# Moving the general expert path: from before the first four of experts, unrolled, to between the fourth and fifth four, as a loop

## The chip, the cores and the metric

The kernel runs on one core of one Trainium2 chip. The metric is the device time of one execution in microseconds (us); three runs of the kernel before gave 936.14, 939.47 and 940.57, median 939.47.

## The reference

A batch of one sequence with 256 tokens of 1024 features passes through two blocks. The first is sparse attention and a gated MLP, merged and projected by `w_out`, and then a mixture of 32 experts:

```
gp = softmax(h @ rg_w + rg_b)                   # best of 4 groups
el = (h @ re_w + re_b)[group]                   # 2 best of its 8 experts
for e in range(32):
    he = silu(h @ w_gate[e]) * (h @ w_up[e])    # 1024 -> 256
    y = y + comb[:, e] * (he @ w_down[e])       # 256 -> 1024
x = rms_norm(x + y)
```

The second block (two layers, each with a gated linear recurrence and a chunked mLSTM) follows on the same `x`. All data is float32. The expert weights alone are 32 x 3 x 1 MiB, read once.

## The kernel before

Only the stage of the experts matters here. The 32 experts are worked through as eight fours, numbered q = 0 to 7 as in the code (so the fourth and fifth four of the title are four 3 and four 4). Each expert of a four has 32 slots for tokens, so a four fills the 128 partitions. For each four:

- `onehot(q)` (L976 to L982, VectorE) writes `oht`, the one-hot matrix that says which token sits in which slot. Its tile has the tag `sOH` and two buffers.
- `gather(q)` (L1027, 32 matmuls) multiplies the tokens `h2h` and `h2l` by `oht`; L1031 and L1032 put the result into `xg`.
- `hidden(q)` (L1129, 64 matmuls with 512 columns on 32-column tiles) multiplies `xg` by the gate and up weights; L1131 and L1132 make `sil`. L1116 to L1120 make the slot weights on VectorE.
- `output(q)` transposes `sil` (L1140), multiplies by the down weights (L1149, 32 matmuls) and scatters into `x1` (L1156 on TensorE, L1158 on VectorE).

The loop at the end writes these as hidden(q), a condition, gather(q + 1), output(q). A scheduler orders each engine's instructions inside a straight piece, so gather(q + 1) and output(q) are interleaved, but nothing moves across a condition. The condition after hidden(q) (L1166, L1167) asks whether an expert of the four has more than 32 tokens; if so, the same four is worked through again with the slots from 32 on. On these inputs that happens once, after hidden(2).

The general path stands ahead of four 0 (L1047 to L1090): if an expert has more than 64 tokens (`CAP`), all 32 experts are applied to the left-over tokens, in code that is unrolled 32 times. Its weight tiles `wf` have the tag `sOH` too. On these inputs no expert has so many tokens: every engine jumps over it. Of a condition each engine has its own branch, and the way past it has a short block of its own, in which the engine raises its semaphores by what the skipped code would have raised them. In SP's block there are eight such steps, one for each of the eight semaphores (lanes, named DMAHW0 to DMAHW7) that its transfers count on in turn; each step waits for the count of all the transfers issued so far on its lane.

The weights are loaded on one queue, SP's, as transfers of 512 KiB. 19 buffers of 1 MiB are used in turn; a four takes 8 for gate and up and 4 for down. `eloads(12 * q + 27)` after the condition of four q refills the 8 buffers that hidden(q) has read, `eloads(12 * q + 31)` after output(q) the 4 of the down weights: 24 transfers in all. They keep the order of the program on SP, and SP's branches stand among them. A transfer is issued when the one eight before it has landed (same lane) and its buffer is free. The 8 buffers of the gate and up weights count as free once TensorE is past the condition of four q, since the repeated four reads them as well. After the last four, `head_load` (L251) loads the first weight chunk of the next block and ScalarE and VectorE split it (L273, L274); that split stands ahead of the last four's output on ScalarE.

Of the kernel before, what the change touches and what calls it, by code (L numbers as in the profile page):

```python
# [19 lines left out]
KT = 8  # L20
# [159 lines left out]
def model(ctx, tc, A, out, dbg=None):  # L180
# [10 lines left out]
    def nm(s):  # L191
        uid[0] += 1
        return f"{s}_{uid[0]}"

    def psum(tag="mm", bufs=4):
        return pp.tile([P, 512], F32, tag=tag, name=nm(tag), bufs=bufs)
# [4 lines left out]
    def psum_t():  # L201
        return psum("tp", 2)

    def f32(ap):
        return ap.bitcast(F32)
# [15 lines left out]
    def vc(name, j=0, n=1):  # L221
        o, _ = _VEC[name]
        return vec[:, o + j:o + j + n]
# [269 lines left out]
    with tc.tile_pool(name="b1", bufs=1) as bp, tc.tile_pool(name="sp1", bufs=3) as sp:  # L493
# [383 lines left out]
        def x1k(i):  # L877

            return x1[:, i, :].rearrange("t (p k) -> t k p", k=KT)
# [85 lines left out]
    with moe, tc.tile_pool(name="mo", bufs=1, reuse_waits="tile") as bp:  # L965
# [53 lines left out]
        def gather(oht, afters=None):  # L1019


            pss = [psum() for _ in range(2)]
            for i in range(2):
                with tc.issue_after(afters[i].ins) if afters else ExitStack():
                    for k in range(KT):
                        for n, part in enumerate((h2h, h2l)):
                            TE.matmul(pss[k // 4][:, P * (k % 4):P * (k % 4) + P], lhsT=part[i][:, k, :], rhs=oht[:, i, :],  # L1027
                                      start=i + n + k % 4 == 0, stop=i + n + k % 4 == 5)
            xg = bp.tile([P, KT, P], F32, tag="xg", name=nm("xg"), bufs=2)
            for k in range(4):  # L1030
                S.activation(out=xg[:, k, :], in_=pss[0][:, P * k:P * k + P], func=AF.Copy, scale=vc("n2gp", k))  # L1031
            V.tensor_tensor(out=xg[:, 4:8, :], in0=pss[1][:].rearrange("p (k t) -> p k t", k=4),  # L1032
                            in1=vc("n2gp", 4, 4).rearrange("p (k o) -> p k o", o=1).to_broadcast([P, 4, P]), op=OP.mult)
            return xg
# [9 lines left out]
        while folds:  # L1044
            ada_fold()

        over = nc.values_load(ovi[0:1, 0:1], min_val=0, max_val=2 * T)  # L1047
        with tc.If(over > CAP):
            cw = bp.tile([P, 256], F32, tag="ohx", name="cw")[:, 0:64].rearrange("p (i e) -> p i e", i=2)
            for i in range(2):  # L1050
                V.tensor_scalar(out=tmp[:, i, :], in0=oh1[:, i, :], scalar1=s4[:, i, 2:3], scalar2=None, op0=OP.mult)
                V.scalar_tensor_tensor(out=cw[:, i, :], in0=oh2[:, i, :], scalar=s4[:, i, 3:4], in1=tmp[:, i, :], op0=OP.mult, op1=OP.add)
            V.tensor_tensor(out=cw, in0=cw, in1=ovm, op=OP.mult)
            hfT = [bp.tile([P, KT, P], F32, name=nm("hfT"), **at) for at in (dict(tag="xg", bufs=2), dict(tag="bc"))]
            for i in range(2):
                for k4 in range(2):
                    pt = psum_t()
                    for k in range(4):
                        TE.transpose(pt[:, k * P:(k + 1) * P], x1k(i)[:, 4 * k4 + k, :], ident)
                    for k in range(4):  # L1060
                        V.tensor_scalar(out=hfT[i][:, 4 * k4 + k, :], in0=pt[:, k * P:(k + 1) * P], scalar1=vc("n2gp", 4 * k4 + k), scalar2=None, op0=OP.mult)
            for e in range(NEXP):
                gus = [psum(), psum()]
                for g, w in enumerate((A["w_gate"], A["w_up"])):
                    for kq in range(4):
                        wf = bp.tile([P, 2, FF], F32, tag="sOH", name=nm("wf"), bufs=2)
                        SY.dma_start(out=wf, in_=w[0, e].rearrange("(p k) c -> p k c", k=KT)[:, 2 * kq:2 * kq + 2, :])
                        for i in range(2):
                            for k in (2 * kq, 2 * kq + 1):
                                TE.matmul(gus[i][:, 256 * g:256 * g + 256], lhsT=hfT[i][:, k, :], rhs=wf[:, k % 2, :], start=k == 0, stop=k == KT - 1)  # L1070
                heTs = []
                for i, gu in enumerate(gus):
                    sil = bp.tile([P, T], F32, tag="sil", name=nm("sil"), bufs=2)
                    S.activation(out=sil, in_=gu[:, 0:256], func=AF.Silu, scale=r2[:, i, 3:4])
                    V.scalar_tensor_tensor(out=sil, in0=gu[:, 256:512], scalar=cw[:, i, e:e + 1], in1=sil, op0=OP.mult, op1=OP.mult)
                    pt = psum_t()
                    for f in range(2):
                        TE.transpose(pt[:, f * P:(f + 1) * P], sil[:, f * P:(f + 1) * P], ident)
                    heT = bp.tile([P, T], F32, tag="heT", name=nm("heT"), bufs=2)
                    V.tensor_copy(heT, pt[:, 0:256])  # L1080
                    heTs.append(heT)
                for n in range(4):
                    wf = bp.tile([P, 2, 256], F32, tag="sOH", name=nm("wf"), bufs=2)
                    SY.dma_start(out=wf, in_=A["w_down"][0, e].rearrange("(f p) c -> p f c", p=P)[:, :, 256 * n:256 * n + 256])
                    for i in range(2):
                        po = psum()
                        for f in range(2):
                            TE.matmul(po[:, 0:256], lhsT=heTs[i][:, f * P:(f + 1) * P], rhs=wf[:, f, :], start=f == 0, stop=f == 1)
                        xs = x1[:, i, 256 * n:256 * n + 256]
                        V.tensor_tensor(out=xs, in0=xs, in1=po[:, 0:256], op=OP.add)  # L1090


        bc = bp.tile([P, 5, T], F32, name="bc")
        s5 = bp.tile([5, T], F32, name="s5")
        pt = psum_t()
# [10 lines left out]
        def hidden(b, xg):  # L1106

            q4, keep = b % NQ, tc.keep_in_program_order if not b else lambda r: r
            ws = loaded["g", q4]

            slot = cc("slot")[:, b:b + 1]
            oa = bp.tile([P, T], F32, tag="oa", name=nm("oa"))
            ohs = bp.tile([P, T], F32R, tag="ohs", name=nm("ohs"), bufs=3)
            wsl = bp.tile([P, 3], F32, tag="wsl", name=nm("wsl"), bufs=2)
            for j in range(2):
                V.scalar_tensor_tensor(out=oa, in0=bc[:, j, :], scalar=slot, in1=bc[:, 2 + j, :], op0=OP.is_equal, op1=OP.mult, accum_out=wsl[:, j:j + 1])  # L1116
            V.tensor_tensor(out=wsl[:, 0:1], in0=wsl[:, 0:1], in1=wsl[:, 1:2], op=OP.add)
            V.tensor_scalar(out=oa, in0=bc[:, 0, :], scalar1=slot, scalar2=None, op0=OP.is_equal)
            V.scalar_tensor_tensor(out=ohs, in0=bc[:, 1, :], scalar=slot, in1=oa, op0=OP.is_equal, op1=OP.add)
            V.scalar_tensor_tensor(out=oa, in0=f32(ohs[:]), scalar=1.0, in1=bc[:, 4, :], op0=OP.mult, op1=OP.mult, accum_out=wsl[:, 2:3])  # L1120
            gu = psum_a()
            for k in range(KT):
                for q in range(4):
                    if q4:
                        w = ws[4 * (k // 4) + q][:].rearrange("p (g k c) -> p g k c", g=2, k=4)[:, :, k % 4, :]
                    else:
                        w = ws[2 * (k // 2) + q // 2][:].rearrange("p (q g k c) -> p q g k c", q=2, g=2, k=2)[:, q % 2, :, k % 2, :]
                    o = slice(SLOTS * q, SLOTS * q + SLOTS)
                    keep(TE.matmul(gu[o, :], lhsT=xg[:, k, o], rhs=w, start=k == 0, stop=k == KT - 1))  # L1129
            sil = bp.tile([P, T], F32, tag="sil", name=nm("sil"), bufs=2)  # L1130
            S.activation(out=sil, in_=gu[:, 0:256], func=AF.Silu, scale=wsl[:, 2:3])  # L1131
            V.scalar_tensor_tensor(out=sil, in0=gu[:, 256:512], scalar=wsl[:, 0:1], in1=sil, op0=OP.mult, op1=OP.mult)  # L1132
            return sil, ohs

        def output(b, sil, ohs, then=None):
# [24 lines left out]
                    then(i)  # L1160
            return r

        for q in range(NQ):
            h = hidden(q, xgs[q])

            more = nc.values_load(ovi[0:1, q + 1:q + 2], min_val=0, max_val=2 * T)  # L1166
            with tc.If(more > SLOTS):  # L1167
                output(NQ + q, *hidden(NQ + q, gather(onehot(NQ + q))))
            if q == NQ - 1:
                break  # L1170
            eloads(12 * q + 27)
            xgs[q + 1] = gather(onehot(q + 1))
            output(q, *h)
            eloads(12 * q + 31)
            if q == NQ - 2:

                first = wtiles()
# [461 lines left out]
```

## Time and profile before

| what | us |
|---|---|
| runs: median (lowest to highest) | 939.47 (936.14 to 940.57) |
| profiled execution: its time, its span | 938.49, 936.8 |
| TensorE busy (share of the span) | 861.4 (92%) |
| VectorE busy | 548.8 (59%) |
| ScalarE busy | 442.2 (47%) |
| SP's hardware queue, share of the 16 DMA engines over the span | 69.1% |
| stage of the experts, hidden(0) to the last output | 235 to 475 of the span |

The span is the time from the first to the last instruction; 1.7 us of the run lie outside. Busy shares are averages over stages with different limits: in the stage of the experts TensorE waits, and the share of the DMA engines is close to 1 for most of it. In the rows below, PE is TensorE's matmuls, PEld its weight loads, DVE is VectorE, ACT ScalarE, SPq the queue of SP's DMA issues; a `q` behind another engine's name is its sequencer, which handles branches and semaphores. PEclk is the granted clock of TensorE as a share of 2.4 GHz: 0.50 is 1.2 GHz.

### The profile page before, as it was taken

What the parts mean: (1) busy time and instruction counts of PE and PEld (TensorE: products, weight loads), DVE (VectorE), ACT (ScalarE), POOL (GpSimd) and SP (SyncE); (2) the same over time, 40 slices, a digit from 0 to 9 for tenths busy, and PEclk for the clock granted to TensorE, in tenths of its full rate; (3) what the DMA queues carried; (4) which work ended last, traced back from release to release, by engine and by line L of the source; (5) the groups of instructions that cost most, each with busy time, mean ns of one, the idle gap of its engine ahead of it and who ended that gap; (6) DMA issues with size and microseconds to landing.
All of it is one profiled execution on the core that took longest, in us unless ns stands there. A gap on an engine that the chain in (4) does not pass through costs nothing.

```text
span 936.8 us, 15106 instructions
## 1 busy us (share of the span) xinstructions
PE 861.4 (92%) x5992; PEld 669.1 (71%) x5992; DVE 548.8 (59%) x1036; ACT 442.2 (47%) x754; POOL 16.6 (2%) x35
## 2 busy tenths in 40 slices
PE   8999999996988888888589999999999999999997
PEld 6888798985334333323169997897778999899776
DVE  5588563863323333312178979357656898835875
ACT  4555853541201111101156787466445779655742
POOL 1000000000000000000000000000100000000100
PEclk9999999995888899999799999999999999999999
DMA  9973749957599989999988645855329854674201
GB/s 314 362 266 123 250 157 328 341 191 272 188 403 398 367 305 385 397 402 405 379 273 272 209 144 180 269 166 195 122 81 329 256 179 136 225 243 162 90 1 45
DMA packets 135288, 229.84 MB, mean 245 GB/s; under 512 B 5920, under 2 KB 78624, under 8 KB 135072
## 3 DMA queue, kind: packets, MB, share of 16 engines
q1 hardware_dynamic: 132400, 225.43, 69.1%
q10 hardware_dynamic: 2800, 3.22, 1.0%
q8 instruction: 57, 0.93, 0.4%
q14 instruction: 31, 0.25, 0.1%
HBM read 226.53 MB, written 2.10 MB: 244 GB/s over the span
## 4 chain that ended last, share of the span: by engine, by line
PE 42%; DVE 3%; ACT 2%; issue 2%; POOL 1%; POOLq 0%; ACTq 0%; DVEq 0%
PE mm L263 11%; PE mm L261 11%; PE mm L262 11%; PE mm L397 2%; PE mm L1398 1%; PE at L1421 1%; PE tp L1431 1%; PE mm L1149 1%; ACT wh L273 1%; DVE wl L274 1%; PE at L263 1%; PE at L261 1%; PE at L262 1%; DVE junk L1254 0%; PE tp L1486 0%
## 5 line engine op out<-in xcount | busy, mean ns | idle before, releaser
L274 DVE TENSOR_TENSOR wl<-w,wh 128x1024 fp32r<-128x1024 f32 x164 | 199.4, 1221 | 116.2 <-ACT wh L273 114.8
L273 ACT ACTIVATE wh<-w 128x1024 fp32r<-128x1024 f32 x164 | 171.7, 1057 | 128.0 <-PE mm L262 60.2
L261 PE MATMUL mm<-hh,wh 128*128 128x256 f32 (+1 forms) x624 | 178.2, 286 | 5.3 <-ACT wh L273 5.3
L263 PE MATMUL mm<-hh,wl 128*128 128x256 f32 (+1 forms) x624 | 178.3, 287 | 0.8 <-DVE wl L274 0.8
L262 PE MATMUL mm<-hl,wh 128*128 128x256 f32 (+1 forms) x624 | 177.1, 284 | 0.4 <-DVE hl L560 0.4
L261 PEld LDWEIGHTS mm<-hh,wh 128*128 128x128 f32 (+1 forms) x624 | 118.6, 190 | 9.2 <-ACT wh L273 6.5
L263 PEld LDWEIGHTS mm<-hh,wl 128*128 128x128 f32 (+1 forms) x624 | 118.3, 190 | 6.0 <-issue 2.9
L262 PEld LDWEIGHTS mm<-hl,wh 128*128 128x128 f32 (+1 forms) x624 | 118.3, 190 | 2.2 <-issue 1.1
L1129 PE MATMUL at<-w,xg 128*32 128x512 f32 x576 | 91.8, 640 | 7.7 <-DMA w<-in_w_up 7.7
L262 PE MATMUL mm<-wl,hh 128*128 128x256 f32 x256 | 72.2, 284 | 0.0
L261 PE MATMUL mm<-wh,hh 128*128 128x256 f32 x256 | 72.1, 287 | 0.0
L263 PE MATMUL mm<-wh,hl 128*128 128x256 f32 x256 | 71.7, 282 | 0.0
L1129 PEld LDWEIGHTS at<-w,xg 128*32 128x32 f32 x576 | 21.0, 116 | 57.2 <-issue 55.4
L1149 PE MATMUL mm<-w,heT 128*32 128x512 f32 x288 | 51.2, 718 | 7.7 <-ACT heT L1142 7.7
L1027 PE MATMUL mm<-oht,h2h 128*128 128x128 f32 x144 | 42.9, 327 | 13.9 <-DVE oht L982 13.9
L1027 PEld LDWEIGHTS mm<-oht,h2h 128*128 128x128 f32 x144 | 34.3, 238 | 26.4 <-issue 15.1
L1131 ACT ACTIVATE sil<-at,wsl 128x256 f32<-128x256 f32 x9 | 4.3, 473 | 101.9 <-PE at L1129 101.9
L261 PEld LDWEIGHTS mm<-wh,hh 128*128 128x128 f32 x256 | 47.6, 188 | 4.3 <-issue 2.5
L262 PEld LDWEIGHTS mm<-wl,hh 128*128 128x128 f32 x256 | 48.6, 190 | 2.5 <-issue 2.3
L263 PEld LDWEIGHTS mm<-wh,hl 128*128 128x128 f32 x256 | 48.3, 189 | 0.9 <-issue 0.8
L1158 DVE TENSOR_TENSOR x<-x,mm 128x512 f32<-128x512 f32 x36 | 23.2, 684 | 36.2 <-PE mm L1156 36.2
L1027 PE MATMUL mm<-oht,h2l 128*128 128x128 f32 x144 | 42.0, 322 | 0.0
(443 smaller groups left out, 1631.3 us busy)
## 6 DMA issues: line engine op xcount, KB each, us to landing
w<-in_w_in SPq DMA_DIRECT2D x55, 1024.0 KB, 7.5
w<-in_w_down SPq DMA_DIRECT2D x64, 512.0 KB, 10.5
w<-in_w_gate SPq DMA_DIRECT2D x56, 512.0 KB, 10.5
w<-in_w_up SPq DMA_DIRECT2D x56, 512.0 KB, 10.6
w<-in_w_ada SPq DMA_DIRECT2D x24, 1024.0 KB, 5.2
w<-in_w_out SPq DMA_DIRECT2D x20, 1024.0 KB, 4.9
w<-in_w_gate SPq DMA_DIRECT2D x16, 256.0 KB, 7.0
w<-in_w_up SPq DMA_DIRECT2D x16, 256.0 KB, 6.9
```

The source lines that it names most:

```text
L261: pin(TE.matmul(o, lhsT=lh, rhs=rh, start=start and k == 0, stop=False))
L262: pin(TE.matmul(o, lhsT=lh, rhs=rl, start=False, stop=False))
L263: pin(TE.matmul(o, lhsT=ll, rhs=rh, start=False, stop=stop and k == nk - 1))
L273: splits[S] = S.activation(out=h, in_=src, func=AF.Copy)
L274: splits[V] = V.tensor_tensor(out=l, in0=src, in1=f32(h), op=OP.subtract)
L397: r = pin(TE.matmul(acc[32 * k:32 * k + 32, :], lhsT=cact[:, hf * 4 + k:hf * 4 + k + 1].to_broadcast([P, 32]), rhs=w[:, k * 512:(k + 1) * ...
L1027: TE.matmul(pss[k // 4][:, P * (k % 4):P * (k % 4) + P], lhsT=part[i][:, k, :], rhs=oht[:, i, :], start=i + n + k % 4 == 0, stop=i + n + k ...
L1129: keep(TE.matmul(gu[o, :], lhsT=xg[:, k, o], rhs=w, start=k == 0, stop=k == KT - 1))
L1149: TE.matmul(po[o:o + SLOTS, :], lhsT=heT[:, f * P + o:f * P + o + SLOTS], rhs=wd[2 * n + q // 2][:, (2 * (q % 2) + f) * 512:(2 * (q % 2) + ...
L1158: V.tensor_tensor(out=xs, in0=xs, in1=ps, op=OP.add)
L1398: TE.matmul(ps[:, 256 * hb:256 * hb + 256], lhsT=xm[:, 2 * h + k, 3 + i * P:3 + (i + 1) * P], rhs=wv[:, (2 * h + k) * 256:(2 * h + k + 1) ...
L1421: TE.matmul(ps[:, 0:256], lhsT=kT[:, 2 * h + k, 0:128], rhs=qT[:, 2 * h + k, :], start=k == 0, stop=k == 1)
```

## The change

The general path leaves its place ahead of four 0 and becomes a function, `general()`, called in the loop between output(3) and hidden(4). Inside the condition it loops over the experts on the engines' own registers instead of being unrolled. Inside it, the token features come from `h2h` and `h2l`, since `x1` holds sums by then, and both feature tiles use the tag `xg`. Because those tiles share their buffers with gather(4), gather(4) is no longer written ahead of output(3) but behind `general()`. Nothing else differs: apart from the general path and the stretch from hidden(3) to hidden(4), every engine's instructions stand in the same order.

```
-        over = nc.values_load(ovi[0:1, 0:1], min_val=0, max_val=2 * T)
-        with tc.If(over > CAP):
...
-            for e in range(NEXP):
-                gus = [psum(), psum()]
...
-                        wf = bp.tile([P, 2, FF], F32, tag="sOH", name=nm("wf"), bufs=2)
-                        SY.dma_start(out=wf, in_=w[0, e].rearrange("(p k) c -> p k c", k=KT)[:, 2 * kq:2 * kq + 2, :])
...
+        def general():
+
+            over = nc.values_load(ovi[0:1, 0:1], min_val=0, max_val=2 * T)
+            with tc.If(over > CAP):
...
+                hfT = [bp.tile([P, KT, P], F32, tag="xg", name=nm("hfT"), bufs=2) for _ in range(2)]
...
+                with tc.For_i(0, NEXP, 1) as e:
...
+                            wf = bp.tile([P, 2, FF], F32, tag="sOH", name=nm("wf"), bufs=2)
+                            SY.dma_start(out=wf, in_=w[0, bass.ds(e, 1)].rearrange("o (p k) c -> p (o k) c", k=KT)[:, 2 * kq:2 * kq + 2, :])
...
         for q in range(NQ):
+            if q == NQ // 2:
+                general()
+                xgs[q] = gather(onehot(q))
             h = hidden(q, xgs[q])
...
             eloads(12 * q + 27)
-            xgs[q + 1] = gather(onehot(q + 1))
+            if q + 1 != NQ // 2:
+                xgs[q + 1] = gather(onehot(q + 1))
             output(q, *h)
             eloads(12 * q + 31)
```

TensorE at the old place, before: between the last matmul of gather(0) and the transpose of the slot table `s` that hidden(0) waits for, there is the load of the register with the count, the branch, and the general path.

```order
L1027 MATMUL mm_2336<-oht_2281,h2h_1969 128x128
L1027 MATMUL mm_2336<-oht_2281,h2l_1971 128x128
L1047 TENSOR_LOAD ovi [waits DVE_49]
L1048 COMPARE_AND_BRANCH
...
L1048 UNCONDITIONAL_BRANCH [waits PE_49]
L1097 MATMUL tp_5834<-cst,s_1966 5x128 [waits DVE_49,PE_49]
```

The same place now (L1051 is the L1097 of before):

```order
L1027 MATMUL mm_2336<-oht_2281,h2h_1969 128x128
L1027 MATMUL mm_2336<-oht_2281,h2l_1971 128x128
L1051 MATMUL tp_2383<-cst,s_1966 5x128 [waits DVE_49,PE_49]
L1051 MATMUL tp_2383<-cst,s_1966 5x128
L1057 MATMUL tp_2387<-s_2382,cst 128x256 [waits DVE_49]
```

The transpose now follows the gather at once.

VectorE between four 3 and four 4, before: it starts behind the condition of four 3; `oht` is the one-hot matrix of four 4, and the L1152 rows belong to output(3).

```order
L976 TENSOR_SCALAR pg_6401<-s_1966 128x4 [waits DVE_49]
L1116 SCALAR_TENSOR_TENSOR oa_6507,wsl_6509<-bc,cst 128x256 [waits DVE_49]
L981 TENSOR_SCALAR ohx_6404<-iota,pg_6401 128x128 [waits DVE_49]
L1116 SCALAR_TENSOR_TENSOR oa_6507,wsl_6509<-bc,cst 128x256 [waits DVE_49]
L982 SCALAR_TENSOR_TENSOR oht_6403<-iota,pg_6401,ohx_6404 128x128 [waits DVE_49]
...
L1152 TENSOR_TENSOR ys_6455<-mm_6457,ys_6455 128x512 [waits Activation_49]
```

The same stretch now, from the last sum of output(3) on (L1112 is the L1158 of before; L1119 and L1120 are the general path's register load and condition):

```order
L1112 TENSOR_TENSOR x_66<-x_66,mm_3649 128x512 [waits PE_49]
L1119 TENSOR_LOAD ovi
L1120 COMPARE_AND_BRANCH
...
L1120 UNCONDITIONAL_BRANCH [waits DVE_49]
L981 TENSOR_SCALAR ohx_3867<-iota,pg_3864 128x128 [waits DVE_49]
L982 SCALAR_TENSOR_TENSOR oht_3866<-iota,pg_3864,ohx_3867 128x128 [waits DMAHW3_49,DMAHW5_49,DMAHW1_49,DMAHW7_49,DVE_49,PE_49]
```

The one-hot matrix of four 4 moved behind output(3) and the condition, and its first write now waits for four of SP's lanes: `oht` takes over a buffer of tag `sOH` that the general path's `wf` would have filled, so the counts that it waits for include the general path's transfers, and when that is skipped, they are raised by SP's block on the way past.

SP between the transfers of four 3 and those of four 4, before (L1167 is the condition of four 4):

```order
L480 DMA w_7162<-in_w_gate 128x1024 [waits DMAHW1_49,PE_49]
L480 DMA w_7162<-in_w_up 128x1024 [waits DMAHW2_49]
L1167 COMPARE_AND_BRANCH
L1167 UNCONDITIONAL_BRANCH x2
L480 DMA w_7364<-in_w_gate 128x1024 [waits DMAHW3_49,PE_49]
```

And now:

```order
L480 DMA w_3662<-in_w_gate 128x1024 [waits DMAHW1_49,PE_49]
L480 DMA w_3662<-in_w_up 128x1024 [waits DMAHW2_49]
L1120 COMPARE_AND_BRANCH
...
L1120 UNCONDITIONAL_BRANCH [waits DMAHW0_49,DMAHW1_49,DMAHW2_49,DMAHW3_49,DMAHW4_49,DMAHW5_49,DMAHW6_49,DMAHW7_49]
L1183 COMPARE_AND_BRANCH
```

SP's branch past the general path, with its waits for all eight lanes, now stands behind the 24 transfers that follow hidden(3); before it stood behind the 19 buffers' first loads, ahead of four 0.

## Rows read from the trace of the kernel before

**Rows 1.** The page's 40 slices of 23.4 us: busy share of the DMA engines, tenths.

```profile
DMA  9973749957599989999988645855329854674201
```

**Rows 2.** Stretches: busy PE, PEld, DVE, ACT, POOL; PEclk, DMA share, GB/s.

```profile
228.00:232.00 4.00, 1.91 (x5) 1.25 (x6) 0.41 (x1) 1.28 (x1) 0.00 (x0) 0.50 0.45 176
232.00:236.00 4.00, 4.00 (x12) 2.21 (x15) 0.84 (x3) 1.58 (x3) 0.00 (x0) 0.50 0.00 0
236.00:240.00 4.00, 4.00 (x36) 1.05 (x32) 1.66 (x8) 1.28 (x1) 0.00 (x0) 0.77 0.02 6
```

**Rows 3.** The old branch L1048: duration ns min/median/max, first and last start.

```profile
L1048 SPq EVENT_SEMAPHORE  x8: 17/17/17, 229.0 to 232.1; - x8
L1048 PEldq COMPARE_BRANCH  x1: 6125/6125/6125, 220.5 to 220.5; - x1
...
L1048 DVEq COMPARE_BRANCH  x1: 76/76/76, 223.9 to 223.9; - x1
...
L1048 DVEq EVENT_SEMAPHORE  x1: 21/21/21, 229.4 to 229.4; - x1
```

**Rows 4.** Timeline from gather(0) to hidden(0): start, duration, what, idle before, releaser.

```profile
223.23 0.69 DVE L1032 TENSOR_TENSOR xg<-mm,vec 128x512 f32<-128x512 f32 x1 [2.40 <-PE mm L1027]
...
229.59 0.58 PE L1097 MATMUL tp<-cst,s 128*5 128x128 f32 x2 [6.40 <-DVEq L1048]
230.68 4.63 PE L1103 MATMUL tp<-s,cst 5*128 5x256 f32 x10 [0.51 <-DVE s L1098]
...
235.24 8.35 PE L1129 MATMUL at<-w,xg 128*32 128x512 f32 x64
```

**Rows 5.** SP's issues at the old place, after hidden(3) and after hidden(4).

```profile
220.32 0.33 SPq L480 DMA_DIRECT2D w<-in_w_up  x1
...
346.85 0.33 SPq L480 DMA_DIRECT2D w<-in_w_gate  x1
...
373.14 0.33 SPq L480 DMA_DIRECT2D w<-in_w_up  x1
374.48 0.33 SPq L480 DMA_DIRECT2D w<-in_w_gate  x1
...
402.08 0.53 SPq L480 DMA_DIRECT2D w<-in_w_up  x1
404.33 0.33 SPq L480 DMA_DIRECT2D w<-in_w_gate  x1
...
406.91 0.33 SPq L480 DMA_DIRECT2D w<-in_w_gate  x1
```

**Rows 6.** DMA issues from 345 to 375: count, size, median us to landing.

```profile
w<-in_w_gate SPq DMA_DIRECT2D x9, 512.0 KB, 10.6
```

**Rows 7.** Timeline of the repeated four: gather, hidden, transpose, last matmuls of the output.

```profile
296.34 0.48 PE L1027 MATMUL mm<-oht,h2h 128*128 128x128 f32 x1 [2.55 <-DVE oht L982]
...
303.36 8.42 PE L1129 MATMUL at<-w,xg 128*32 128x512 f32 x64
...
312.90 0.44 PE L1140 MATMUL tp<-cst,sil 128*128 128x128 f32 x2 [1.13 <-DVE sil L1132]
...
317.38 2.54 PE L1156 MATMUL mm<-ys,ohs 128*128 128x512 f32 x8
```

**Rows 8.** Timeline: the last 32 matmuls of hidden(3) and of hidden(4).

```profile
341.75 3.64 PE L1129 MATMUL at<-w,xg 128*32 128x512 f32 x32
...
365.63 3.64 PE L1129 MATMUL at<-w,xg 128*32 128x512 f32 x32
```

**Rows 9.** What the matmuls of L1129 waited for: us in total, times.

```profile
  DMA w<-in_w_up: 7.7, 7
```

**Rows 10.** Timeline from the last hidden to the last output.

```profile
451.17 0.67 SPq L251 DMA_DIRECT2D w<-in_w_in  x1
...
464.14 2.00 ACT L273 ACTIVATE wo<-w 128x1024 fp32r<-128x1024 f32 x2 [8.66 <-DMA w<-in_w_ada]
...
466.47 5.35 PE L1149 MATMUL mm<-w,heT 128*32 128x512 f32 x32 [7.26 <-ACT heT L1142]
```

More of the change, by code (lines that the diff above doesn't have):

```diff
@@ L1045, in model @@
             ada_fold()
-        over = nc.values_load(ovi[0:1, 0:1], min_val=0, max_val=2 * T)
-        with tc.If(over > CAP):
[L1049 to L1061, printed above, removed]
-            for e in range(NEXP):
-                gus = [psum(), psum()]
-                for g, w in enumerate((A["w_gate"], A["w_up"])):
-                    for kq in range(4):
-                        wf = bp.tile([P, 2, FF], F32, tag="sOH", name=nm("wf"), bufs=2)
-                        SY.dma_start(out=wf, in_=w[0, e].rearrange("(p k) c -> p k c", k=KT)[:, 2 * kq:2 * kq + 2, :])
[L1068 to L1090, printed above, removed]
@@ L1161, in output @@
             return r
+        def general():
+            over = nc.values_load(ovi[0:1, 0:1], min_val=0, max_val=2 * T)
+            with tc.If(over > CAP):
+                cw = bp.tile([P, 256], F32, tag="ohx", name="cw")[:, 0:64].rearrange("p (i e) -> p i e", i=2)
+                for i in range(2):
+                    V.tensor_scalar(out=tmp[:, i, :], in0=oh1[:, i, :], scalar1=s4[:, i, 2:3], scalar2=None, op0=OP.mult)
+                    V.scalar_tensor_tensor(out=cw[:, i, :], in0=oh2[:, i, :], scalar=s4[:, i, 3:4], in1=tmp[:, i, :], op0=OP.mult, op1=OP.add)
+                V.tensor_tensor(out=cw, in0=cw, in1=ovm, op=OP.mult)
+                hfT = [bp.tile([P, KT, P], F32, tag="xg", name=nm("hfT"), bufs=2) for _ in range(2)]
+                for i in range(2):
+                    for k4 in range(2):
+                        n2 = vc("n2gp", 4 * k4, 4).rearrange("p (k o) -> p k o", o=1).to_broadcast([P, 4, P])
+                        for part in (h2h, h2l):
+                            pt = psum_t()
+                            for k in range(4):
+                                TE.transpose(pt[:, k * P:(k + 1) * P], f32(part[i][:, 4 * k4 + k, :]), ident)
+                            o = hfT[i][:, 4 * k4:4 * k4 + 4, :]
+                            p4 = pt[:].rearrange("p (k t) -> p k t", k=4)
+                            if part is h2h:
+                                V.tensor_copy(o, p4)
+                            else:
+                                V.tensor_tensor(out=o, in0=p4, in1=o, op=OP.add)
+                                V.tensor_tensor(out=o, in0=o, in1=n2, op=OP.mult)
+                ce, cwe = small(1, "ce"), small(1, "cwe")
+                V.tensor_scalar(out=ce, in0=gmx, scalar1=0.0, scalar2=1.0, op0=OP.mult, op1=OP.add)
+                with tc.For_i(0, NEXP, 1) as e:
+                    for i in range(2):
+                        V.scalar_tensor_tensor(out=tmp[:, i, :], in0=iota[:, 0:32], scalar=ce[:, i, :], in1=cw[:, i, :], op0=OP.is_equal, op1=OP.mult, accum_out=cwe[:, i, :])
+                    V.tensor_scalar(out=ce, in0=ce, scalar1=1.0, scalar2=None, op0=OP.add)
+                    gus = [psum(), psum()]
+                    for g, w in enumerate((A["w_gate"], A["w_up"])):
+                        for kq in range(4):
+                            wf = bp.tile([P, 2, FF], F32, tag="sOH", name=nm("wf"), bufs=2)
+                            SY.dma_start(out=wf, in_=w[0, bass.ds(e, 1)].rearrange("o (p k) c -> p (o k) c", k=KT)[:, 2 * kq:2 * kq + 2, :])
+                            for i in range(2):
+                                for k in (2 * kq, 2 * kq + 1):
+                                    TE.matmul(gus[i][:, 256 * g:256 * g + 256], lhsT=hfT[i][:, k, :], rhs=wf[:, k % 2, :], start=k == 0, stop=k == KT - 1)
+                    heTs = []
+                    for i, gu in enumerate(gus):
+                        sil = bp.tile([P, T], F32, tag="sil", name=nm("sil"), bufs=2)
+                        S.activation(out=sil, in_=gu[:, 0:256], func=AF.Silu, scale=r2[:, i, 3:4])
+                        V.scalar_tensor_tensor(out=sil, in0=gu[:, 256:512], scalar=cwe[:, i, :], in1=sil, op0=OP.mult, op1=OP.mult)
+                        pt = psum_t()
+                        for f in range(2):
+                            TE.transpose(pt[:, f * P:(f + 1) * P], sil[:, f * P:(f + 1) * P], ident)
+                        heT = bp.tile([P, T], F32, tag="heT", name=nm("heT"), bufs=2)
+                        V.tensor_copy(heT, pt[:, 0:256])
+                        heTs.append(heT)
+                    for n in range(4):
+                        wf = bp.tile([P, 2, 256], F32, tag="sOH", name=nm("wf"), bufs=2)
+                        SY.dma_start(out=wf, in_=A["w_down"][0, bass.ds(e, 1)].rearrange("o (f p) c -> p (o f) c", p=P)[:, :, 256 * n:256 * n + 256])
+                        for i in range(2):
+                            po = psum()
+                            for f in range(2):
+                                TE.matmul(po[:, 0:256], lhsT=heTs[i][:, f * P:(f + 1) * P], rhs=wf[:, f, :], start=f == 0, stop=f == 1)
+                            xs = x1[:, i, 256 * n:256 * n + 256]
+                            V.tensor_tensor(out=xs, in0=xs, in1=po[:, 0:256], op=OP.add)
```

## The prediction

> **What bounds the kernel now.** I read the page's slices first, then the stage of the experts by timeline and by SP's issues. The slices show the DMA engines full in the second half of that stage [rows 1]: from about 351 to 468 us every slice is a 9. So the question for each part of the change is whether it moves the stream of weights, not whether TensorE gets less to do. The stream has no slack at its end: the matmuls of hidden wait for weights seven times, 7.7 us in all [rows 9], and the last output cannot start before the next block's first chunk has landed, since ScalarE splits that chunk first. It is issued at 451.17, the split starts at 464.14, the last L1149 at 466.47 [rows 10]. What delays the stream after 347 us delays the end of the kernel by as much; what advances the whole stage is a gain by as much.
>
> **The old place: what goes.** After gather(0) TensorE stands idle for 6.40 us and names VectorE's L1048 as the releaser [rows 4]. That is the jump over the unrolled path: TensorE's branch takes 6.1 us, and VectorE's next step comes at 229.4 after a branch at 223.9, 5.5 us later [rows 3]. Nothing else is in that gap; `s` was long ready. Now the transpose follows the gather. Its copy on VectorE has to wait for L1032, which ends at 223.92, so about 0.15 us of the gap stays and the stage starts 6.25 us earlier. The clock may add something: it is 0.50 of 2.4 GHz in the slices up to 236 and rises in 236 to 240, with TensorE at work since 230.68 after the long gap [rows 2, 4]. Without that gap it may rise earlier: 64 matmuls at the full clock take 2 x 3.64 = 7.28 us [rows 8] against the 8.35 of hidden(0), and half of the 4.63 of L1103 would go as well. The bounds are 6.2 and 6.25 + 1.07 + 2.3 = 9.6 us; I take 6.8, near the lower end, because how early the clock rises is open. Weights don't hold this: SP's loads before were issued by 220.32, the DMA engines were idle from about 230, and the next loads came only behind hidden(0). So hidden(0) to hidden(3) and all loads between them shift rigidly by 6.8 us.
>
> One rule of the Trainium skill speaks against this term: "Advanced Engine Details and Errata", section Control Flow Timing, gives a compare-and-branch about 108 ns. By it the gap would not belong to the branch, the move would give back next to nothing, and the sum below would be some 6.8 us higher, near 960. Another page, "Runtime: NRT & Kernel Launch", section Instruction fetch mechanics, says that a taken branch to a target outside the fetched window must fetch it first; the trace agrees with that one, with 5.5 us on VectorE [rows 3].
>
> **The new place: what comes.** I give times on the clock of before and take off the 6.8 us at the end.
>
> 1. Hidden(3) ends at 341.75 + 3.64 = 345.39 [rows 8]. SP then issues the 24 transfers, the first at 346.85, the 24th at 373.14 [rows 5]. That is as before.
> 2. Next on SP stands the way past the general path, which waits on all eight lanes, so for every transfer in flight. How long: at the old place the last issue was at 220.32 and the eighth step of SP's block at 232.1, 11.8 us later [rows 3, 5]; the median landing here is 10.6 us [rows 6]. I take 11.3: SP gets through at 384.4. In before no such stop exists here; SP issued the 25th transfer at 374.48.
> 3. Output(3) now has no gather beside it. In the repeated four it took from the end of hidden, 303.36 + 8.42 = 311.78, to 317.38 + 2.54 = 319.92, so 8.1 us [rows 7]: TensorE is done at 353.5. Behind it stands gather(4), which needs `oht`, whose first write waits for the lanes that SP raises at 384.4. TensorE, VectorE and ScalarE have nothing else to do and stand for about 31 us. Their own jumps past the general path fall into that time and cost nothing, even at 6 us each; so does SP's, whose waiting covers it. Without that cover each would cost up to 6.
> 4. `oht` and the first matmul: 0.4 us (296.34 against the end of hidden is a longer chain, so this is an estimate from a 0.35 us write). Gather and hidden of the repeated four took 311.78 - 296.34 = 15.4 us, begun at the low clock [rows 7]. After 31 us of standing I expect the same: hidden(4) ends at 400.2, against 365.63 + 3.64 = 369.27 before [rows 8].
> 5. The next loads need the buffers of hidden(4), and SP follows the end of a hidden by 346.85 - 345.39 = 1.46 us: the 25th transfer goes out at 401.7. The DMA engines have been empty since about 382 (at the old place they were done by 229.8, 0.45 of the slice from 228 [rows 2], and SP by 232.1).
> 6. From there the stream runs again. From an empty queue 24 issues took 374.48 - 346.85 = 27.6 us, so the 49th goes out at 429.3, against 406.91 before: 22.4 us late [rows 5]. Before, SP was held once on that way (2.25 us from 402.08 to 404.33, where 1.3 is usual), which a late stream is spared: 21.5.
>
> After that TensorE has spare time. A four takes it about 24 us (345.39 to 369.27), so hidden(7) could end at 400.2 + 3 x 23.9 = 471.9 while the late stream brings the next block's chunk at 464.1 + 21.5 = 485.6. The stream remains the bound, and the delay reaches the end in full.
>
> **The sum.** -6.8 + 21.5 = +14.7 us on the profiled 938.49, so 953.2; that execution lies 1 us under the median of the three, and I predict 953. For the ends: if hidden(4) runs at the full clock (gather half of 303.36 - 296.34 = 7.0, so 3.5 less, hidden 1.1 less), SP drains in 10.6 and the gain at the top is 9.6, then 21.5 - 4.6 - 0.7 - 9.6 = +6.6, or 945. If the jump is paid a second time behind the drain (6.1) and the top gives only 6.2, then 22.4 + 6.1 - 6.2 = +22.3, or 961.
>
> **Rivals.**
>
> *The wait is met early: faster.* If the counts that `oht` waits for stand before TensorE is through with output(3), at 353.5, nothing drains and TensorE pays only what the new order exposes: 8.1 us of output, 1 to 2 us of branch and one-hot, 15.4 us of gather and hidden. Hidden(4) then ends near 371, 2 us later than before, which the stream hides because SP reaches its 25th transfer only at 374.48. The 6.8 us stay: 931.7. It decides at one point: SP past L1120 before 353.5. For it speaks that SP passed the conditions of the fours without any wait before. Against it speaks the order: 24 transfers stand ahead, the last issued at 373.14.
>
> *Only SP stops: no change.* If VectorE is let through although SP still drains, hidden(4) ends near 371 and its buffers are free. SP goes on at 384.4 from an empty queue, the 49th issue comes at 384.4 + 27.6 = 412.0, 5.1 late: 938.5 + 5.1 - 6.8 = 936.8. For it speaks that four lanes, not eight, are named on VectorE; against it that the raising of all the eight stands in one block, and that the first step there waits for the transfers issued last.
>
> *More than forecast.* TensorE starved or slowed after the restart, or the jump paid behind the drain: 958 to 961.
>
> **How the numbers follow.** Forecast 0.84, met early 0.06, only SP 0.06, more than forecast 0.04. What a measurement here can tell from no change is about 0.5%, 4.7 us, so 934.8 and 944.2 are the bounds. All of the forecast and the last rival lie above 944.2: slower 0.88. Only SP gives no change: same 0.06, faster 0.06. The range of the forecast by its ends is 945 to 961; single runs of the kernel before differ by 4 us, so I give 944 to 960. The two cases below it hold 0.12, and some 0.03 are above.
>
> **What would show it.** In the new trace: no idle of 6 us between gather(0) and the transpose, and hidden(0) about 7 us earlier. Between output(3) and gather(4) an idle of TensorE of about 30 us, ended by `oht`, with VectorE's write waiting for a lane; SP's L1120 steps some 11 us behind the last of the 24 issues; the DMA engines empty for about 20 us right after; gather(4) at 1.2 GHz. From there to the last output more waits for weights in hidden(6) and hidden(7). I am wrong if SP passes L1120 while transfers are in flight, if TensorE's idle there is under 10 us, or if the stage of the experts ends earlier than at 475.

## The result, and the profile after

| | us |
|---|---|
| kernel before: median of its runs (lowest to highest) | 938.01 (936.14 to 940.57) |
| changed kernel: median of four runs (lowest to highest) | 950.21 (949.40 to 954.06) |
| ratio of the times, 95% interval | 1.0136 (1.0096 to 1.0176) |
| profiled execution after: its time, its span | 949.70, 948.0 |

The change costs 12.2 us by the medians and 11.2 us by the two profiled executions. The forecast was 953, with a range of 944 to 960.

The slices of the page after: busy share of the DMA engines (tenths, 23.7 us each):

```profile
DMA  9983849935999996499997645854429953674201
```

The 6 and the 4 among the nines are the slices from 356 to 403 us; before, every slice in that stretch is a 9 [rows 1].

TensorE at the old place, timeline after (start, duration, what, idle before and its releaser):

```profile
220.46 0.41 PE L1027 MATMUL mm<-oht,h2l 128*128 128x128 f32 x1
220.67 0.63 PE L1051 MATMUL tp<-cst,s 128*5 128x128 f32 x2
221.97 4.63 PE L1057 MATMUL tp<-s,cst 5*128 5x256 f32 x10 [0.68 <-DVE s L1052]
226.53 9.80 PE L1083 MATMUL at<-w,xg 128*32 128x512 f32 x64
```

The 6.40 us are gone [rows 4]: the transpose follows the gather. Hidden(0) takes 9.80 us where it took 8.35. The windows of the same stretch after (busy PE, PEld, DVE, ACT, POOL; PEclk, DMA share, GB/s) say why:

```profile
228.00:232.00 4.00, 4.00 (x24) 0.98 (x20) 1.02 (x4) 1.28 (x1) 0.00 (x0) 0.50 0.01 3
232.00:236.00 4.00, 4.00 (x40) 0.96 (x32) 0.00 (x0) 0.00 (x0) 0.00 (x0) 0.99 0.01 4
```

More of hidden(0) ran at 1.2 GHz: the clock is 0.50 up to 232 us, 5.5 us into hidden(0). Before, it rose about 3 us into it (0.57 from 237 to 238, 1.00 from 238 to 239; hidden(0) starts at 235.24 [rows 4]). From the end of gather(0) to the end of hidden(0) it is 236.33 - 220.87 = 15.5 us, against 243.59 - 223.19 = 20.4 before.

The new place. The condition L1120 after (duration ns min/median/max, first and last start):

```profile
L1120 SPq EVENT_SEMAPHORE  x8: 17/17/17, 370.4 to 373.2; - x8
...
L1120 PEldq COMPARE_BRANCH  x1: 330/330/330, 344.7 to 344.7; - x1
...
L1120 DVEq COMPARE_BRANCH  x1: 56/56/56, 345.6 to 345.6; - x1
L1120 DVEq EVENT_SEMAPHORE  x1: 21/21/21, 346.6 to 346.6; - x1
L1120 SPq COMPARE_BRANCH  x1: 45/45/45, 363.1 to 363.1; - x1
...
  DVE oht L982: 26.4, 1
```

The engines are past it within about 1 us. SP arrives at 363.1 and is through with its eight steps at 373.2; VectorE's `oht` waits 26.4 us for that. SP's issues after: the first and 24th behind hidden(3), the 25th, and the next block's first chunk:

```profile
337.14 0.33 SPq L480 DMA_DIRECT2D w<-in_w_gate  x1
...
362.68 0.33 SPq L480 DMA_DIRECT2D w<-in_w_up  x1
390.47 0.34 SPq L480 DMA_DIRECT2D w<-in_w_gate  x1
...
462.59 0.70 SPq L251 DMA_DIRECT2D w<-in_w_in  x1
```

Between the 24th and the 25th lie 27.8 us; before, they were 1.3 apart [rows 5]. The timeline after, from hidden(3) to hidden(4):

```profile
333.35 3.64 PE L1083 MATMUL at<-w,xg 128*32 128x512 f32 x32
...
344.24 0.97 PE L1110 MATMUL mm<-ys,ohs 128*128 128x512 f32 x3 [0.15 <-DVE ys L1106]
...
373.39 0.35 DVE L982 SCALAR_TENSOR_TENSOR oht<-iota,pg,ohx 128x128 fp32r<-128x128 f32 x1 [26.38 <-SPq L1120]
...
373.89 0.44 PE L1027 MATMUL mm<-oht,h2h 128*128 128x128 f32 x1 [28.67 <-DVE oht L982]
...
380.87 9.43 PE L1083 MATMUL at<-w,xg 128*32 128x512 f32 x64
```

One chain: SP's last step releases `oht`, `oht` releases gather(4), the end of hidden(4) at 390.3 frees the buffers, and 0.16 us later SP issues the 25th transfer. Meanwhile the DMA engines stand empty (windows after, columns as above):

```profile
370.00:374.00 4.00, 0.11 (x1) 0.14 (x1) 0.58 (x2) 0.00 (x0) 0.00 (x0) 0.50 0.32 127
374.00:378.00 4.00, 4.00 (x20) 4.00 (x20) 0.41 (x2) 0.00 (x0) 0.00 (x0) 0.50 0.01 4
...
386.00:390.00 4.00, 4.00 (x44) 0.96 (x32) 0.00 (x0) 0.00 (x0) 0.00 (x0) 1.00 0.02 4
390.00:394.00 4.00, 1.55 (x14) 1.04 (x10) 2.87 (x13) 0.86 (x2) 0.00 (x0) 1.00 0.58 206
```

The delay reaches the end of the stage: ScalarE's split of the next chunk starts at 475.09 and the last output at 477.41, against 464.14 and 466.47 [rows 10].

```profile
475.09 2.00 ACT L273 ACTIVATE wo<-w 128x1024 fp32r<-128x1024 f32 x2 [9.67 <-DMA w<-in_w_in]
...
477.41 1.08 PE L1103 MATMUL mm<-w,heT 128*32 128x512 f32 x4 [5.45 <-ACT heT L1096]
```

The profiled execution after is already 2.3 us ahead when gather(0) ends (220.87 against 223.19), in a part that the change does not touch. So the stretches below are measured from an event of the same execution: D is the time from the end of hidden(3) to the issue of the next block's first chunk, 105.8 us before and 125.6 after. Single runs of the kernel before lay between 931.8 and 945.0, so what a placing is worth is read from medians and ratios.

### The profile page after: what moved, and what is told of

It is laid out like the page before. It is cut to its first block, busy times and chain, and to the rows that moved or that the text cites. A ratio compares the mean times of both kernels' runs of the same rounds, so it can differ in the third digit from the quotient of the medians.

```text
span 948.0 us, 15105 instructions
## 1 busy us (share of the span) xinstructions
PE 858.5 (91%) x5992; PEld 671.6 (71%) x5992; DVE 548.8 (58%) x1036; ACT 441.0 (47%) x753; POOL 16.6 (2%) x35
## 5 line engine op out<-in xcount | busy, mean ns | idle before, releaser
L1083 PE MATMUL at<-w,xg 128*32 128x512 f32 x576 | 86.5, 652 | 1.5 <-DMA w<-in_w_up 1.5
L1027 PE MATMUL mm<-oht,h2h 128*128 128x128 f32 x144 | 45.2, 340 | 38.8 <-DVE oht L982 38.8
L261 PE MATMUL mm<-wh,hh 128*128 128x256 f32 x256 | 72.1, 287 | 0.0
L1083 PEld LDWEIGHTS at<-w,xg 128*32 128x32 f32 x576 | 19.8, 118 | 49.0 <-issue 46.7
L1103 PE MATMUL mm<-w,heT 128*32 128x512 f32 x288 | 48.4, 705 | 6.5 <-ACT heT L1096 6.5
L1031 ACT ACTIVATE xg<-mm,vec 128x128 f32<-128x128 f32 x36 | 10.3, 369 | 80.5 <-PE mm L1027 80.5
L1027 PE MATMUL mm<-oht,h2l 128*128 128x128 f32 x144 | 44.8, 336 | 0.0
```

Of the source, the lines that this page charges most:

```text
L261: pin(TE.matmul(o, lhsT=lh, rhs=rh, start=start and k == 0, stop=False))
L1103: TE.matmul(po[o:o + SLOTS, :], lhsT=heT[:, f * P + o:f * P + o + SLOTS], rhs=wd[2 * n + q // 2][:, (2 * (q % 2) + f) * 512:(2 * (q % 2) + ...
```

## The experiments

The theory: the skipped path's transfers count on SP's lanes, so SP, on its way past, waits for every transfer in flight; `oht` waits for SP, and the buffers that the stream needs wait for `oht`. The main rivals: the drained queue alone, the late gather(4), or the length of the jump.

| kernel | D, us | median, us | ratio to before, 95% |
|---|---|---|---|
| changed kernel | 125.6 | 950.2 | 1.0136 (1.0096 to 1.0176) |
| unrolled at the new place | 125.8 | 951.5 | 1.0177 (1.0125 to 1.0228) |
| general path at two places | (see below) | 974.5 | 1.0404 (1.0352 to 1.0455) |
| `wf` in buffers of its own | 108.8 | 932.7 | 0.9982 (0.9950 to 1.0014) |
| transfers on GpSimd's queue | 103.9 | 931.0 | 0.9920 (0.9890 to 0.9950) |
| no general path, late gather(4) | 102.7 | 930.1 | 0.9922 (0.9892 to 0.9953) |
| no general path, gather(4) as before | 104.4 | 929.0 | 0.9917 (0.9887 to 0.9947) |
| loop at the old place | 103.0 | 933.0 | 0.9937 (0.9910 to 0.9965) |
| behind the condition of four 3 | 106.1 | 933.3 | 0.9971 (0.9940 to 1.0001) |
| the same, on GpSimd's queue | 103.7 | 931.4 | 0.9938 (0.9914 to 0.9961) |
| behind the condition of four 0 | 104.3 | 935.3 | 0.9973 (0.9942 to 1.0003) |

Each ratio is to runs of the kernel before taken alongside, whose median was 938.0 for the changed kernel and 936.4 to 936.8 for the others. D comes from one execution each. From hidden(3) on, the kernel before, the loop at the old place and the kernel with no general path and gather(4) as before hold the same code, and their D is 105.8, 103.0 and 104.4: differences under 3 us say nothing.

**Take away `oht`'s wait, keep SP's stop.**

```
-  wf = bp.tile([P, 2, FF], F32, tag="sOH", name=nm("wf"), bufs=2)
+  wf = bp.tile([P, 2, FF], F32, tag="wf", name=nm("wf"), bufs=2)     # and at the second place
```

> One tag is changed in the changed kernel: the general path's weight tiles get buffers of their own, so that the one-hot matrix of four 4 no longer takes over a buffer of theirs and its write waits for no lane. SP's stop at the general path stays. My theory (SP's drain costs so much because the one-hot matrix waits for it too, so that the fifth four's hidden layer and the buffers it frees come late): TensorE's idle ahead of gather(4) falls from 28.7 us to under 4, hidden(4) ends some 20 us earlier than in the changed kernel, SP still gets past the condition about 10.5 us behind its 24th issue, the 25th transfer goes out at about 373 to 375 of the span instead of 390.5, and the time is 934 to 941 us, against 950.2 for the changed kernel and 938 for the kernel before. Rival A (the drained queue by itself is what costs, whoever else waits): still 947 to 952. Rival B (the later place of gather(4) is what costs): the idle before gather(4) goes, but hidden(4) still ends over 10 us late and the time stays over 945.

L1120 and SP's 24th and 25th issue in this kernel, and TensorE at gather(4):

```profile
L1120 SPq EVENT_SEMAPHORE  x8: 17/17/17, 367.1 to 369.9; - x8
```

```profile
358.96 0.33 SPq L480 DMA_DIRECT2D w<-in_w_up  x1
370.26 0.34 SPq L480 DMA_DIRECT2D w<-in_w_gate  x1
```

```profile
343.81 0.30 PE L1027 MATMUL mm<-oht,h2h 128*128 128x128 f32 x1 [2.34 <-DVE oht L982]
```

SP still drains, 10.9 us behind its 24th issue (369.9 - 358.96), and goes on at once, since hidden(4) has long ended. The time is 932.7, a little under the expected 934 to 941, and the 25th issue 3 us earlier than expected. So of the 125.6 us of D, 16.8 hang on `oht` waiting for SP, and the drain by itself is worth 108.8 - 103.9 = 4.9 against the kernel on GpSimd's queue. By the ratios the parts are 0.0154 and 0.0062, about 14 and 6 us; the intervals of this kernel and of the one on GpSimd's queue just touch, so that the drain costs something can be told, and how much only roughly. Rivals A and B fall.

**Take away SP's stop**, and with it `oht`'s wait for SP.

```
-  SY.dma_start(out=wf, in_=w[0, bass.ds(e, 1)]...)
+  nc.gpsimd.dma_start(out=wf, in_=w[0, bass.ds(e, 1)]...)            # and for w_down
```

> The changed kernel with the general path's weight transfers issued by GpSimd instead of SP; loop, place, tiles and tags stay as in the changed kernel. SP then issues nothing inside the condition and has nothing to stop for; the one-hot matrix of four 4 waits for GpSimd's way past the condition. My theory (the price is the drain of the queue that carries the stream, because the skipped code's transfers count on its lanes): SP has no steps at the general path's condition, TensorE's idle ahead of gather(4) falls from 28.7 us to under 4, the 25th transfer goes out at most 29 us behind hidden(3)'s end (53.5 in the changed kernel), and the time is 928 to 936 us. Rival (whatever waits at a skipped path with transfers costs about the same, on any queue): 945 or more. Rival (the later place of gather(4) costs): 938 to 945; the kernel without general path that kept the late gather(4) speaks against it with 930.1.

L1120 in this kernel, gather(4), and SP's 24th and 25th issue:

```profile
L1120 POOLq EVENT_SEMAPHORE  x4: 17/42/43, 221.1 to 221.4; - x4
```

```profile
345.55 0.30 PE L1027 MATMUL mm<-oht,h2h 128*128 128x128 f32 x1 [2.40 <-DVE oht L982]
```

```profile
360.86 0.33 SPq L480 DMA_DIRECT2D w<-in_w_up  x1
362.67 0.33 SPq L480 DMA_DIRECT2D w<-in_w_gate  x1
```

GpSimd takes its steps from 221.1 to 221.4, over 100 us before anyone asks. SP has no steps there at all. Place, loop, tags and order are those of the changed kernel, and it takes 931.0 us, 19 less.

**The new order by itself**: `general()` is not called; gather(4) stays behind output(3).

> The changed kernel without the general path: neither its condition nor its body is there, but the one-hot matrix and gather(4) stay behind output(3) as in the changed kernel. So it holds the new order of the fifth four by itself, without any stop on SP. My theory (the order is hidden by the stream of weights): hidden(4) ends 2 to 5 us later against hidden(3) than in the kernel before, SP issues its 25th transfer at most 3 us later against hidden(3), and the time is 930 to 936 us, that of a kernel without general path. Rival (the exposed output(3) and gather(4) cost their length): 8 to 16 us more, 940 to 948.

**The bound**: neither the general path nor the late gather(4).

> The changed kernel without the general path, neither condition nor body, and with gather(4) written beside output(3) as in the kernel before. It is the bound: what any placing of the general path could at best give. My theory: 928 to 934 us, the same within 2 us as the kernel without general path and with the late gather(4) (930.1). Rival (the exposed order costs several us): 4 to 8 us below that one, 922 to 926.

930.1 and 929.0, with intervals that nearly coincide: the late gather(4) costs nothing that can be told here. One point of the expectation was wrong in its sign: hidden(4) ends 358.51 - 339.77 = 18.7 us behind hidden(3), against 23.9 before, so it is earlier by itself, since it no longer runs between the steps of output(3): from its first matmul to its end it takes 358.51 - 351.44 = 7.1 us, where before it took 11.9. Against the changed kernel, the first one puts the price of the skipped path at its new place at 1.0136 - 0.9922 = 0.0214 of some 937 us, 20 us.

**The length of the jump at the new place**: the body unrolled 32 times again.

```
-  with tc.For_i(0, NEXP, 1) as e:
+  for e in range(NEXP):
```

> The changed kernel with the general path unrolled 32 times again instead of looped, at the new place; all else as in the changed kernel. My theory (at the new place the jump is covered by SP's drain): SP's eight steps come at the same 10 to 12 us behind the 24th issue, the engines' jumps grow from 0.3 to 1 us to about 6 us inside TensorE's idle, and the time is that of the changed kernel, 947 to 953 us. Rival (the length of the jump is paid at the new place): 954 to 958, by one more fetch of about 6 us behind the drain.

L1120 in this kernel, and gather(4):

```profile
L1120 PEldq COMPARE_BRANCH  x1: 6039/6039/6039, 344.6 to 344.6; - x1
L1120 DVEq COMPARE_BRANCH  x1: 56/56/56, 345.6 to 345.6; - x1
L1120 PEldq EVENT_SEMAPHORE  x1: 51/51/51, 350.7 to 350.7; - x1
L1120 DVEq EVENT_SEMAPHORE  x1: 21/21/21, 351.3 to 351.3; - x1
```

```profile
374.94 0.45 PE L1027 MATMUL mm<-oht,h2h 128*128 128x128 f32 x1 [29.77 <-DVE oht L982]
```

The jumps are back at 6 us and lie inside an idle of 29.8. D is the same within 0.2 us.

**The loop at the old place**, nothing moved:

> The kernel before with its general path written as a loop, at its old place ahead of four 0; gather(4) is interleaved with output(3) again. It is the half of the change that shortens the path without moving it. My theory (the 6.4 us at the old place is the length of the jump over unrolled code): TensorE's idle between gather(0) and the transpose falls from 6.4 us to between 0.5 and 2.5 us, and the time is 929 to 936 us, 2 to 6 us below the kernel before. Rival (a taken branch costs the same whatever it jumps over): the idle stays at 5 to 6.5 us and the time at 934 to 940, no change.

The condition is L1050 in this kernel; behind it TensorE's transpose:

```profile
L1050 PEldq COMPARE_BRANCH  x1: 5997/5997/5997, 220.9 to 220.9; - x1
...
L1050 DVEq COMPARE_BRANCH  x1: 72/72/72, 224.3 to 224.3; - x1
L1050 DVEq EVENT_SEMAPHORE  x1: 21/21/21, 224.5 to 224.5; - x1
```

```profile
227.28 0.59 PE L1112 MATMUL tp<-cst,s 128*5 128x128 f32 x2 [3.71 <-PEq L1050]
```

Half a miss. VectorE's way past the condition fell from 5.5 us to 0.2, but TensorE's stayed at 6.0, and the gap is now TensorE's own: 3.71, between the two expectations. The time, 933.0, is in the range of the theory. So the old gap had two owners that ended at 226.6 and 229.4 [rows 3]; the loop removes the later one alone.

**An empty queue instead of a full one**: the call stands right behind the condition of four 3, and in another kernel of four 0; gather(4) is beside output(3) again.

```
             eloads(12 * q + 27)          # ahead of this line:
+            if q == 3:                   # the other kernel: q == 0
+                general()
```

> The looped general path is called at another place: right behind the condition of four 3, ahead of the 24 transfers that hidden(3) sets free, so that SP meets its stop when its queue has long been empty; the one-hot matrix and gather(4) are written beside output(3) again, and the general path's silu tile has a tag of its own. My theory (what counts is what is in flight when SP comes to the stop): SP gets past the condition within 1 us of hidden(3)'s end, since the loads before have landed; the one-hot matrix still names lanes but waits under 1 us; TensorE has no idle over 4 us there; the stream goes on as in the kernel before, and only the gain at the old place is left: 930 to 936 us, faster than the kernel before by 0.3 to 0.9%. Rival A (a skipped general path costs by itself, wherever it stands in the loop): 945 or more. Rival B (the jump over the path, on engines with no cover here, costs about 6 us each time, so what the old place gives back is paid again): 936 to 940.

> The looped general path called right behind the condition of four 0, otherwise like the kernel that has it behind the condition of four 3. There the weight buffers were last filled long before and the queue is empty, but one transfer is issued ahead of SP's stop, and the loads behind it can't start until it has landed. My theory: SP's steps end 3 to 5 us behind that issue, the stream of the second four starts 3 to 5 us later, the jumps on the engines are short (0.3 to 2.5 us), and the time is 931 to 938 us, up to 5 above the kernel without general path. Rival (the loop inside the fours costs as at the place of the change, some 15 to 20 us): 945 or more.

SP's first two issues behind that condition, with four 3, and then with four 0:

```profile
340.11 0.33 SPq L480 DMA_DIRECT2D w<-in_w_gate  x1
344.19 0.34 SPq L480 DMA_DIRECT2D w<-in_w_up  x1
```

```profile
236.57 0.33 SPq L480 DMA_DIRECT2D w<-in_w_gate  x1
240.04 0.34 SPq L480 DMA_DIRECT2D w<-in_w_up  x1
```

In both the scheduler put one transfer ahead of the condition, so SP waits for that one to land: 4.1 and 3.5 us, not the under 1 us that I expected behind four 3. The times are in the expected ranges, 933.3 and 935.3, and the rivals at 945 or more fall; the second time is 6 above the bound, a little more than the 5 allowed. By their intervals neither kernel can be told from the kernel before.

**Both repairs**: behind the condition of four 3, on GpSimd's queue.

> The looped general path right behind the condition of four 3, with gather(4) beside output(3), and the general path's weight transfers issued by GpSimd: the two repairs together. My theory: SP makes no stop, the first of the 24 transfers goes out within 1.6 us of hidden(3)'s end and the next at once, what is left is TensorE's jump (2.4 us at this place before), and the time is 928 to 933 us, that of the kernel without general path within 2 us. Rival (the jump on the engines, and not SP's stop, was what this place cost): 932 to 935 as with SP's transfers.

931.4, 2.4 above the bound where I had allowed 2: SP's second issue follows 0.54 us behind the first, and what is left is TensorE's jump of 2.67 us. By the intervals it can't be told from the kernel with GpSimd's queue at the new place.

**Twice the cost**: `if q in (4, 6)` in place of `if q == NQ // 2`.

> The changed kernel with the general path at two places: between output(3) and hidden(4) as in the changed kernel, and once more, by the same code, between output(5) and hidden(6), with gather(6) behind it as well. The suspected cost is doubled. My theory (each skipped copy behind a full queue costs one drain and one restart): at the second copy SP's eight steps end 10 to 12 us behind the 24th issue, TensorE's idle ahead of gather(6) is 25 to 30 us, and the time rises by 16 to 22 us above the changed kernel, to 966 to 972. Rival (the first drain uses up the slack, the second meets a queue that runs behind and costs little): under 8 us more, 950 to 958.

L1120 and gather(6) in this kernel:

```profile
L1120 SPq EVENT_SEMAPHORE  x16: 17/17/17, 367.5 to 455.2; - x16
```

```profile
455.80 0.44 PE L1027 MATMUL mm<-oht,h2h 128*128 128x128 f32 x1 [33.08 <-DVE oht L982]
```

The second copy does the same again: SP is through 10.9 us behind its 24th issue (444.28), TensorE idles 33 us. It costs 24.3 us, more than the 16 to 22 expected. The chunk of the next block goes out at 482.91, before hidden(7) starts at 483.56: so late in the stage, it seems, there is no long stream left behind which TensorE's own delay could hide; no run tests that reason. The rival falls.

## Why the prediction was right

- **What bounds it.** The stream from 347 us on does: what delayed it (D +19.8) reached the end of the stage. The chunk went out 11.4 us later in the span (462.59 against 451.17), which is 19.8 less the 8.4 by which hidden(3) ended earlier, and its split started 10.95 later.
- **Old place, -6.8.** The gap went, and hidden(0) to hidden(3) came earlier with it, though not rigidly. Counted from the end of gather(0), the profiled execution is 4.9 us earlier at the end of hidden(0) and 6.1 at the end of hidden(3) (116.1 against 122.2). By the ratios, the kernel without general path and with the late gather(4) is 0.9922 of before, -7.3 us (-4.4 to -10.1), over the whole execution. The bonus from the clock was taken with the wrong sign: it rose later against hidden(0), not earlier, and hidden(0) ran 1.45 us longer.
- **Why the gap was there** the forecast had half right. For VectorE it was the length of the skipped code: 5.5 us unrolled at the old place, 5.7 unrolled at the new place, 0.2 looped at the old place. TensorE's branch took 6.0 us over the loop at the old place too, so its part does not follow from the unrolling. The figure of the Trainium skill for a compare-and-branch, about 108 ns ("Advanced Engine Details and Errata", Control Flow Timing), does not hold for these branches. Its rule that a taken branch outside the fetched window must fetch first ("Runtime: NRT & Kernel Launch", Instruction fetch mechanics) would fit VectorE's 5.5 and 0.2 us, but no run here shows a fetch.
- **Step 2, the drain.** Through 11.3 us behind the last issue by the forecast; measured 10.5 (373.2 - 362.68).
- **Step 3.** Output(3) 8.1 us, measured 345.21 - 336.99 = 8.2; TensorE's idle 31, measured 28.7, ended by `oht`, with the engines' own jumps inside it.
- **Step 4.** `oht` and the first matmul 0.4, measured 0.7 from SP's last step at 373.2; gather and hidden, begun at the low clock, 15.4, measured 390.31 - 373.89 = 16.4.
- **Steps 1 and 5** were sized too high: SP followed the ends of hidden(3) and hidden(4) by 0.15 and 0.16 us, not by 1.46. The 1.46 was no property of SP. Its first issue waits until TensorE is past the condition of four 3, and TensorE's branch there, over the short code of one repeated four, took 3.65 us before and 0.44 after (before, then after):

```profile
L1167 PEldq COMPARE_BRANCH  x1: 3651/3651/3651, 343.1 to 343.1; - x1
L1183 PEldq COMPARE_BRANCH  x1: 435/435/435, 334.7 to 334.7; - x1
```

Before, the branch ended at 346.75, and SP issued at 346.85 [rows 5]. The forecast's errors partly cancel, which is luck: 1.3 too much in each of steps 1 and 5, 0.8 in the drain and 0.7 in the 24 issues ahead of it, 1.3 too little in step 4. Together they put the 25th transfer 53.5 us behind the end of hidden(3), against 29.1 before: 24.4 late, where the forecast had 27.2.
- **Step 6.** From the 25th issue to the chunk it is 462.59 - 390.47 = 72.1 us against 451.17 - 374.48 = 76.7: the late stream made up 4.6. The forecast had 5.7, the 4.8 by which 24 issues from an empty queue are shorter and the 0.9 of the hold at 402. One sign of the forecast came out the other way: it expected more waits for weights after the restart, and hidden waited for gate and up weights 2.6 us in four waits after, against 8.8 in ten before. (The 7.7 us that the forecast gives as all of it are the up weights alone [rows 9].) Before, the line that follows the one of [rows 9], and after:

```profile
  DMA w<-in_w_gate: 1.1, 3
```

```profile
  DMA w<-in_w_up: 1.9, 2
  DMA w<-in_w_gate: 0.7, 2
```

- **The sum.** New place +21.5 by the forecast, +19.8 by D; old place -6.8, measured -6.1; together +14.7, measured +13.7. The profiled executions differ by only 11.2 because the one after was already 2.3 ahead at gather(0). So of the 3 us between 953.2 and 950.2 one is an error of the terms, and the rest is of the size by which executions differ elsewhere.
- **The rivals, each under its own condition.** "Met early" said 931.7; with the wait moved to GpSimd's queue it is 931.0. "Only SP stops" said 5.1 us late against before and 936.8; with `oht` freed D is 3.0 longer than before (4.9 longer than on GpSimd's queue) and the time 932.7, so it was sized somewhat too high. What kept them from happening in the changed kernel is what the order showed: SP's steps stand behind 24 transfers, and `oht` waits for lanes.

## What to carry to other kernels

A conditional block that is never entered still costs its place on every queue it would have used: ask which queue its transfers count on, what is in flight there when the condition comes, and who waits for those counts through a shared buffer. Put such transfers on a queue that is idle at that point; here that alone turned 950.2 into 931.0 us, 0.8% under the kernel before. Buffers shared with skipped code are a wait as well, and here that was the larger part: 16.8 of the 21.7 us of D that GpSimd's queue saved. No run here enters the general path, so what GpSimd's queue costs when it is taken is not shown.

## What the runs showed that I had not expected

The same looped code took TensorE a jump of very different length: 0.33 us in the changed kernel, 0.42 with GpSimd's queue, 0.86 behind the condition of four 0, 2.45 and 2.67 behind that of four 3, 6.00 at the old place. Unrolled it took 6.04 and 6.13. TensorE's branch past the short repeated four varied as much: in its seven skips in the kernel before it took 0.32 to 6.20 us. The length of the code alone does not set it; what does, no run here tells apart.

The granted clock fell here after short stops of TensorE. After output(3) of the kernel with GpSimd's queue TensorE waited 2.40 us, and in the middle of gather(4) it stopped for another 1.96, for which the profile shows no releaser; from 348 us the clock is 0.50, and gather(4) and hidden(4) take 17.0 us (345.55 to 362.51). In the kernel with the late gather(4) and no condition there are no such stops, the clock stays at 1.00, and the same work takes 10.7 us (347.82 to 358.51). In these two the stream hid the difference: 931.0 and 930.1. First of them GpSimd's queue (timeline, window), then the other one (timeline):

```profile
348.81 0.27 PE L1027 MATMUL mm<-oht,h2h 128*128 128x128 f32 x1 [1.96 <-issue]
```

```profile
348.00:352.00 4.00, 3.19 (x16) 3.19 (x16) 0.00 (x0) 0.11 (x1) 0.00 (x0) 0.50 1.05 389
```

```profile
351.44 7.07 PE L1083 MATMUL at<-w,xg 128*32 128x512 f32 x64
```
